# Weight-block sums issued behind the up projection's splits, and the last tile's mean behind the next tile's addition

## The chip, the cores and the metric

The kernel runs on one core of one Trainium2 chip. A core has five engines that each work through their own queue of instructions in order: PE (TensorE, matrix products), DVE (VectorE), ACT (ScalarE), POOL (GpSimd) and SP (SyncE, which here only issues transfers). They meet at semaphores. Transfers run on the core's 16 DMA engines; most are issued from SP's queue, some from POOL's and a few from ACT's. The metric is the device time of one execution in microseconds (us), as the median of several runs.

## The reference

One layer of a diffusion backbone over 512 latent tokens with 256 context tokens, model width 1024. What the change touches is the weights of the last part, the gated feed-forward network, and the final norm:

```python
def conv_ffn(h, w_up, conv_w, conv_b, w_down):
    u = dwconv_centred(h @ w_up, conv_w, conv_b)
    a, b = u[..., :D_FF], u[..., D_FF:]
    return (jax.nn.silu(a) * b) @ w_down
...
x = x + gt1 * o_lat
x = x + gt2 * conv_ffn(modulate(x, norm2_g[l], sh2, sc2), w_up[l], ...)
...
return rmsnorm(x, final_g)
```

`D_FF` is 2816, so `w_up` has 44 columns of 128-wide tiles (22 for `a`, 22 for `b`) and `w_down` has 22 rows of them. Ahead of it lie the modulation (six vectors from `silu(c) @ w_mod`), a combined input projection, a Mamba-2 scan in two directions, windowed attention of 16 heads, and the merge of both branches.

## The kernel before

**Products.** Every large product is made in float32r (a reduced form of float32 that PE takes at full rate) from operands that are split in two: `hi` is the rounded copy, `lo` the rest. `split` (L180) makes them from a raw weight tile: ACT casts `raw` to `hi` (L181), DVE subtracts to get `lo` (L182). `gemm` (L225) then issues three matmuls for each 128-row piece: hi with the operand's hi (L231), hi with its lo (L232), lo with its hi (L234). A weight tile of 128 x 1024 is 512 KB and 24 matmuls of 512 columns.

**Order of the stages.** The first norm and the input projection (0 to some 90 us) are followed by attention (to some 340 us), the scan (to some 700), the merge and the output projection (to some 870), the up projection (to some 1107), and the down projection to the end. In attention a planner writes out the order of PE, ACT and DVE by hand; its `product_atoms` (L1058) fill gaps with further input-projection tiles, whose split is `high` (ACT, L1081) and `low` (DVE, L1084). Elsewhere `run` (L204) walks a list of steps: for each it loads and splits the tiles of the steps ahead (`load`, L186), then calls the step. Weight tiles come through three raw buffers (`wraw`), two `whi` and two `wlo`.

**The up projection.** `up_step(t)` for t = 0 to 21 uses tile `("up", t)` for the gated half and `("up", 22 + t)` for the other, and applies the three-tap convolution and the gate (L1384 to L1386, L1892 to L1902). Between these steps `run` weaves in the last eight modulation tiles (`msteps[24:]`): they come through the same raw buffers, and DVE multiplies them by the conditioning vector straight from there (L787, L789). Others in between turn the residual stream around in memory for the last norm (`x1_turn`, L1950 and L1953, and `x1_load`, L1964).

**The down projection.** It is a product of two-by-two blocks, done with seven block products instead of eight (`down_step(j, u)`, j = 0 to 6). Four of the seven take not a block of `w_down` but a sum of blocks. These sums are made in device memory by transfers alone, `SUMS` at L149: for each of `DSUMS[4]`, `[1]`, `[2]`, `[5]`, in this order, four copies of 704 KB and then four accumulating transfers that add another block on top; two of the copies' sets read an earlier sum. They are issued from POOL's queue.

```python
    def sum_step(ins, n=1):

        for _ in range(min(n, len(SUMS))):
            o, x, how = SUMS.pop(0)
            dma = G.dma_start(o, x, **how)
            tc.add_manual_dep(dma.ins, ins.ins.name, BEHIND, reason="weight sums behind a split")
```

`sum_step` (L158) issues the next n of these 32 transfers and makes POOL wait for the instruction `ins`. Before the change, `ins` is the DVE subtraction of the g-th tile that fills attention (L1084): one transfer each for g = 0 to 3, two each for g = 4 to 11, one each for g = 12 to 23. The products that use the sums are j = 1 (`DSUMS[1]`), 2 (`[2]`), 3 (`[5]`) and 4 (`[4]`).

**The end.** The final norm is made for two tiles of 128 tokens, i = 0 and 1, out of the last block product. `near_last(i)` (L2066) multiplies each half of the product by its gate (L2070), adds it to the residual stream (L2072), has ACT square and sum it (L1996), and then takes the mean (`mean_root`: L2038 on DVE, a power on POOL, L2039). `near_out(i)` (L2076) scales (L2078 on ACT, L2082 on DVE) and stores. DVE and ACT keep the order written in `down_step`: near_last(0), near_last(1), near_out(0), near_out(1).

Of the kernel before, what the change touches and what calls it, by code (L numbers as in the profile page):

```python
# [13 lines left out]
ALU = mybir.AluOpType  # L14
# [10 lines left out]
NFF = 22  # L25
# [14 lines left out]
def raw(ap):  # L40
    return ap.bitcast(F32)
# [3 lines left out]
def tile_hybrid_layer(  # L45
# [32 lines left out]
    V, S, G, T = nc.vector, nc.scalar, nc.gpsimd, nc.tensor  # L78
# [28 lines left out]
    def accb():  # L107
        return bank("acc")

    def misb():  # L110
        return bank("mis")
# [3 lines left out]
    def tmp(tag):  # L115
        return tpool.tile([P, 512], F32, tag=tag, name=tag, bufs=TMP[tag])
# [27 lines left out]
    for j, t in enumerate((wdn[0], DSUMS[1], DSUMS[2], DSUMS[5], DSUMS[4], wdn[1], wdn[3])):  # L144
        for u in range(DU):
            n = min(2, DK - 2 * u) * HC
# [11 lines left out]
# [6 lines that stand above are left out]
# [3 lines left out]
    def load_raw(key):  # L167
        a, n = src[key]
        if key[0] == "dn" and key[1] >= 4 and key[1] % 2:
            if "dnraw" not in F:  # L170
                F["dnraw"] = hpool.tile([P, 4, 1024], F32, tag="hlh", name="dnraw")
            r = F["dnraw"][:, key[1] // 2 % 4, :]
        else:
            r = wpool.tile([P, 1024], F32, tag="raw", name="wraw", bufs=3)
        dma = nc.sync.dma_start(r[:, :n], a)
        if key[0] == "m":
            M_LOADS[key[1]] = dma
        return r, n

    def split(r, n, hi, lo):  # L180
        S.copy(hi[:, :n], r[:, :n])  # L181
        return V.tensor_tensor(lo[:, :n], r[:, :n], raw(hi[:, :n]), ALU.subtract)  # L182
# [3 lines left out]
    def load(key):  # L186
        r, n = load_raw(key)
        if key[0] == "m":
            return r
        if key in ELSEWHERE:  # L190
            hi, lo = ELSEWHERE[key]()
            split(r, n, hi, lo)
            return hi, lo
        if key[0] == "dn" and key[1] % 4 > 1:
            if "dnw" not in F:
                F["dnw"] = hpool.tile([P, 2, 2, 1024], F32R, tag="hll", name="dnw")
            hi, lo = (F["dnw"][:, key[1] % 2, i, :] for i in range(2))
        else:
            hi = wpool.tile([P, 1024], F32R, tag="whi", name="whi", bufs=2)
            lo = wpool.tile([P, 1024], F32R, tag="wlo", name="wlo", bufs=2)  # L200
        split(r, n, hi, lo)
        return hi, lo

    def run(prog, early=None):  # L204

        seq = [k for keys, _ in prog for k in keys]
        have, nload, nuse = {}, 0, 0
        for keys, fn in prog:
            nuse += len(keys)
            ahead = 1 + (early in keys) + any(k[0] == "dn" for k in keys)  # L210
            while nload < min(nuse + ahead, len(seq)):
                have[seq[nload]] = load(seq[nload])
                nload += 1
            fn(*[have.pop(k) for k in keys])
# [104 lines left out]
    class Plan:  # L319
# [6 lines left out]
        def add(self, name, engine, cost, needs, rank, emit, whole=True, load=0.11, late=False):  # L326


            self.atoms[name] = dict(
                name=name, engine=engine, cost=cost, needs=needs, rank=rank, emit=emit, whole=whole, load=load,  # L330
                late=late, start=None,
            )
# [86 lines left out]
    with tc.tile_pool(name="spool", bufs=1) as sp:  # L419
# [155 lines left out]
        def product(j, i, t):  # L575
            h = (hi_.get(j), lo_.get(j)) if j < NU else (hlh[:, j, :], hll[:, j, :])

            n = 3 * NU if j < NU else 3 * KT
            part(pg[i], ("P", i), n, [w[j][:, i * P : (i + 1) * P] if j in w else None for w in (wh, wl)], h, t)
# [75 lines left out]
        r = {}  # L655
        cq = tmp("te")[:, :LC]
        for j in range(KT):
# [46 lines left out]
            x = ("hi", "lo") if j >= NU else ("hh", "hl")  # L704
# [31 lines left out]
        for n in range(2):  # L736
            for j in range(KT):
                x = ("hi", "lo") if j >= NU else ("hh", "hl")
# [131 lines left out]
    Q, F = {}, {}  # L870
# [187 lines left out]
    def product_atoms(g, key, accs):  # L1058

        kind, t = key  # L1060
        d, R, G_ = {}, 1e6 + 100 * g, "%d" % g
# [19 lines left out]
            S.copy(d["w"][0], d["r"])  # L1081

        def low():
            sum_step(V.tensor_tensor(d["w"][1], d["r"], raw(d["w"][0]), ALU.subtract), 1 + (4 <= g < 12))  # L1084

        def rope_part(f):
            scale = -0.125 if kind == "k" else 1.0
# [37 lines left out]
        rw = R - 2e6 if g != 1 else -500  # L1125
        atom("w" + G_, "ACT", 1.05, was, rw, high, late=g > OLD)
        atom("v" + G_, "DVE", 1.225, ["w" + G_], rw, low, late=g > OLD)
        ks = range(-4 if kind == "k" else 0, 8)
        for k in ks:
# [31 lines left out]
        f = (q_high, q_low) if kind == "q" else (k_high, k_low)  # L1161
# [486 lines left out]
    for g in range(4):  # L1648
        s = ssd_steps(g)
        f = fill[n2 + g : n2 + 1 + g]  # L1650
        b = proj_steps(g + 1) if g < 3 else fill[n2 + 4 : n3]
# [104 lines left out]
    HL = L // 2  # L1756
    HALF = [slice(0, HL), slice(HL, L)]
# [110 lines left out]
    def f_split(s, ks, x):  # L1868
        S.copy(F["s"][s][:, 0, ks, :], x)
        V.tensor_tensor(F["s"][s][:, 1, ks, :], x, raw(F["s"][s][:, 0, ks, :]), ALU.subtract)  # L1870
# [99 lines left out]
    rows_ = {}  # L1970
# [17 lines left out]
    TWO = range(2)  # L1988

    def xq(h, i, c, z=slice(0, HC)):  # L1990

        return F["xt"][h][:, i, HC * c + z.start : HC * c + z.stop]

    def square_sum(h, i, col_, x):
        sq = tmp("ta")[:, : x.shape[-1]]
        S.activation(sq, x, AF.Square, scale=1.0 / 32.0, accum_out=ss[:, 2 * h + i, col_ : col_ + 1])  # L1996
# [39 lines left out]
    def mean_root(h, i, a, b, e):  # L2036
        ms, rs = (cpool.tile([P, 4], F32, tag=n, name=n, bufs=2)[:, 0:1] for n in ("ms", "rs"))
        V.scalar_tensor_tensor(ms, a, e, b, ALU.add, ALU.add)  # L2038
        G.tensor_tensor(rs, ms, phalf[:, 0:1], ALU.pow)  # L2039
        return rs  # L2040
# [22 lines left out]
        for i in TWO:  # L2063
            V.tensor_scalar_add(ss[:, i, 0:1], ss[:, i, 0:1], EPS)

    def near_last(i):  # L2066
        ps = F["A"][i]
        for b, z in enumerate(HALF):
            t = tmp("ta")[:, :HL]
            V.tensor_tensor(t, ps[:, z], rows_["g"][1][:, z], ALU.mult)  # L2070
            x = xq(0, i, 1, z)
            V.tensor_tensor(x, x, t, ALU.add)  # L2072
            square_sum(0, i, 1 + b, x)
        F["near", i] = mean_root(0, i, ss[:, i, 1:2], ss[:, i, 2:3], ss[:, i, 0:1])

    def near_out(i):  # L2076
        rs, r = F["near", i], P * i
        S.activation(F["p1"][i], F["p1"][i], AF.Copy, scale=rs)  # L2078
        S.dma_start(out[r : r + P, 0:HC], F["p1"][i])
        for z in HALF:  # L2080
            x = xq(0, i, 1, z)
            V.scalar_tensor_tensor(x, x, rs, rows_["f"][1][:, z], ALU.mult, ALU.mult)  # L2082
            nc.sync.dma_start(out[r : r + P, HC + z.start : HC + z.stop], x)
# [20 lines left out]
    def down_step(j, u):  # L2104
        tail = j == 6 and u == DU - 2

        def fn(*w):
            w = {u + n: x for n, x in enumerate(w)}
            if u == 0:
                if j == 0:  # L2110
                    F["A"] = [misb() for _ in TWO]
                F["ps", j] = F["A"] if j in CHAIN else [accb() for _ in TWO]
            ks = range(2 * u, DK if tail else min(2 * u + 2, DK))
            if tail:
                for i in TWO:
                    product(j, i, w, ks)
                with tc.manual_schedule(engines={mybir.EngineType.DVE, mybir.EngineType.Activation}):
                    for f in (near_last, near_out):
                        for i in TWO:
                            f(i)  # L2120
                return
            for k in ks:
                for i in TWO:
                    product(j, i, w, (k,))
            if 1 <= j < 6 and u < 4:
                z = slice(3 * u, min(3 * u + 3, DK))
                f_split((j + 1) % 2, z, OPERAND[j + 1]()[:, z, :])
            BESIDE_DOWN.get((j, u), lambda: None)()

        return [("dn", DU * j + u + n) for n in range(1 + tail)], fn  # L2130
# [99 lines left out]
```

## Time and profile before

| | |
|---|---|
| median of 3 runs | 1226.17 us (1224.75 to 1228.8) |
| the profiled execution's own time | 1223.88 us |
| its span from first to last instruction | 1222.1 us |
| granted TensorE clock | 0.998 of full speed |
| all transfers | 211.55 MB, mean 173 GB/s |
| of these POOL's queue (the 32 sums) | 23.07 MB, 8.5% of the 16 engines' span |
| SP's and ACT's queue q1 | 186.83 MB, 48.8% |

Times in a profile are counted from the start of the span. A row of a timeline is: start, duration, engine, line, operation, what it writes and reads, shape, and in brackets how long the engine had been idle and what released it. `SPq` and `POOL L162` rows of the kind DMA_DIRECT2D are issues of transfers: the duration is that of the issue, and a row "DMA to landing us min/median/max" tells how long the chosen transfers took from issue to landing. Rows of the form "A <- B: total, times, longest" tell how long engine A was idle until B released it.

### The profile page before, as it was taken

To read this page: it belongs to the slowest core of one execution; us is meant where nothing else is said; L and a number is where in the kernel's file an instruction comes from. 1 tells how busy PE (TensorE), PEld (TensorE's weight loads), DVE (VectorE), ACT (ScalarE), POOL (GpSimd) and SP (SyncE) were. 2 spreads that over 40 slices of the span, in tenths; PEclk is the share of its full clock that TensorE was granted. 3 is DMA by queue.
4 is the path that set the end of the run, shared out by engine and by line. 5 is a ranking of instruction groups with operands and counts; after the bars stand their busy time and mean duration, and the time that the engine had idled before them with its cause. 6 is when DMAs were issued, how large, how long until landed. Compare 5 with 4: busy or idle time off the path is not lost.

```text
span 1222.1 us, 17422 instructions
## 1 busy us (share of the span) xinstructions
PE 1210.9 (99%) x6310; PEld 994.8 (81%) x6310; DVE 919.6 (75%) x1481; ACT 682.7 (56%) x1275; POOL 196.2 (16%) x187
## 2 busy tenths in 40 slices
PE   9999999999999999999999999999999999999996
PEld 6798888888878877778777778888988888888885
DVE  5857888888654598697896868577787777777786
ACT  5658788787444467486575663223543434335653
POOL 0000121101000043352451631000200000000053
PEclk9999999999999999999999999999999999999999
DMA  9645789844754435346365568777266533347852
GB/s 372 255 137 183 160 252 256 173 153 125 174 160 151 129 104 176 109 133 195 102 176 194 159 214 273 230 249 224 56 149 162 167 107 103 120 125 181 290 162 87
DMA packets 122551, 211.55 MB, mean 173 GB/s; under 512 B 26720, under 2 KB 69024, under 8 KB 122464
## 3 DMA queue, kind: packets, MB, share of 16 engines
q1 hardware_dynamic: 111280, 186.83, 48.8%
q0 software_dynamic: 10752, 23.07, 8.5%
q8 instruction: 50, 0.82, 0.3%
q10 hardware_dynamic: 432, 0.53, 0.1%
q14 instruction: 37, 0.30, 0.1%
HBM read 185.68 MB, written 42.28 MB: 187 GB/s over the span
## 4 chain that ended last, share of the span: by engine, by line
PE 95%; ACT 1%; DVE 1%; POOL 1%; issue 1%; DMA 0%; POOLq 0%; DVEq 0%; ACTq 0%
PE acc L231 20%; PE acc L234 20%; PE acc L232 20%; PE score L951 3%; PE po L1000 3%; PE pt L987 2%; PE mis L573 2%; PE mis L1604 2%; PE mis L1497 2%; PE mis L2102 1%; PE mis L2100 1%; PE mis L2101 1%; PE mis L1612 1%; PE acc L1070 1%; PE acc L1072 1%; PE acc L1071 1%
## 5 line engine op out<-in xcount | busy, mean ns | idle before, releaser
L181 ACT CAST whi<-wraw 128x1024 fp32r<-128x1024 f32 (+1 forms) x115 | 120.3, 1047 | 157.4 <-PE acc L232 113.3
L231 PE MATMUL acc<-hlh,whi 128*128 128x512 f32 x472 | 194.1, 411 | 0.0
L182 DVE TENSOR_TENSOR wlo<-wraw,whi 128x1024 fp32r<-128x1024 f32 (+1 forms) x115 | 144.1, 1253 | 64.4 <-ACT whi L181 61.0
L232 PE MATMUL acc<-hll,whi 128*128 128x512 f32 x472 | 185.0, 392 | 0.0
L234 PE MATMUL acc<-hlh,wlo 128*128 128x512 f32 x472 | 185.0, 392 | 0.0
L231 PE MATMUL acc<-mh,whi 128*128 128x512 f32 x368 | 143.4, 390 | 0.0
L232 PE MATMUL acc<-ml,whi 128*128 128x512 f32 x368 | 143.2, 389 | 0.0
L234 PE MATMUL acc<-mh,wlo 128*128 128x512 f32 x368 | 143.2, 389 | 0.0
L234 PEld LDWEIGHTS acc<-hlh,wlo 128*128 128x128 f32 x472 | 88.6, 188 | 19.5
L231 PEld LDWEIGHTS acc<-hlh,whi 128*128 128x128 f32 x472 | 88.8, 188 | 17.9 <-issue 3.1
L232 PEld LDWEIGHTS acc<-hll,whi 128*128 128x128 f32 x472 | 88.9, 188 | 17.4 <-issue 2.4
L234 PEld LDWEIGHTS acc<-mh,wlo 128*128 128x128 f32 x368 | 69.1, 188 | 14.5
L231 PEld LDWEIGHTS acc<-mh,whi 128*128 128x128 f32 x368 | 69.1, 188 | 14.3
L232 PEld LDWEIGHTS acc<-ml,whi 128*128 128x128 f32 x368 | 69.1, 188 | 14.1
L1385 DVE SCALAR_TENSOR_TENSOR ta<-acc,half,ta 128x511 f32<-128x511 f32 (+1 forms) x66 | 43.9, 665 | 26.4 <-ACT ta L1384 26.0
L960 DVE CUSTOM_DVE_ANT_0 p<-score,winm,nsink 128x512 f32<-128x512 f32 (+1 forms) x64 | 51.9, 810 | 15.3 <-PE score L951 13.8
L1384 ACT ACTIVATE ta<-acc,half 128x512 f32<-128x512 f32 (+1 forms) x66 | 46.8, 709 | 22.8 <-PE acc L234 21.6
L967 ACT ACTIVATE p<-p,mneg 128x512 f32<-128x512 f32 (+1 forms) x64 | 49.7, 778 | 15.4 <-DVE mneg L960 14.8
L162 POOL DMA_DIRECT2D dsum<-wdn x24 | 25.4, 1143 | 193.0 <-DVE wlo L1084 171.7
L1499 POOL TENSOR_TENSOR st<-st,eT 128x512 f32<-128x512 f32 x24 | 29.7, 1239 | 165.4 <-ACT st L1516 152.0
L231 PE MATMUL acc<-hch,whi 128*128 128x256 f32 x176 | 54.7, 311 | 0.0
L995 DVE TENSOR_TENSOR ptl<-pt,pth 128x512 fp32r<-128x512 f32 x72 | 47.5, 685 | 8.5 <-ACT pth L991 7.9
(426 smaller groups left out, 2998.7 us busy)
## 6 DMA issues: line engine op xcount, KB each, us to landing
wraw<-wup SPq DMA_DIRECT2D x44, 512.0 KB, 3.6
dsum<-wdn POOLq DMA_DIRECT2D x24, 704.0 KB, 9.0
fb<-cs_d SPq DMA_DIRECT2D x32, 512.0 KB, 6.3
wraw<-wm SPq DMA_DIRECT2D x32, 512.0 KB, 3.7
wraw<-wx SPq DMA_DIRECT2D x24, 512.0 KB, 3.5
wm<-wm SPq DMA_DIRECT2D x16, 512.0 KB, 8.0
wraw<-wz SPq DMA_DIRECT2D x16, 512.0 KB, 3.6
wraw<-wos SPq DMA_DIRECT2D x16, 512.0 KB, 4.6
```

What stands on the lines that cost most here:

```text
L181: S.copy(hi[:, :n], r[:, :n])
L182: return V.tensor_tensor(lo[:, :n], r[:, :n], raw(hi[:, :n]), ALU.subtract)
L231: T.matmul(ps, wh, xh[:, k0 + k, :], start=a, stop=False)
L232: T.matmul(ps, wh, xl[:, k0 + k, :], start=False, stop=False)
L234: T.matmul(ps, wl, xh[:, k0 + k, :], start=False, stop=b)
L951: T.matmul(ps[:, o : o + len(z) * P], Q[h][:, b * P : (b + 1) * P], k[:, j, z[0] * P : (z[-1] + 1) * P], start=v == 0 and o % 512 in (0, P ...
L960: V.tensor_tensor_reduce(p[:, :w], d["ps"][i][:, o0 : o0 + w], m, op0=ALU.add, op1=ALU.min, scale=1.0, scalar=nsink[:, h : h + 1], accum_o ...
L967: S.activation(p, p, AF.Exp, bias=d["mneg"][:, i : i + 1], scale=-1.0, accum_out=d["den"][:, i : i + 1])
L995: V.tensor_tensor(d["ptl"][x], d["pt"][x], raw(d["pth"][x]), ALU.subtract)
L1000: T.matmul(d["po"], vst[:, cols[x], j, :], d[y][x], start=x == 0 and y == "pth", stop=x == c - 1 and y == "ptl")
L1384: S.activation(o[:, :n], ps[:, :n], AF.Identity, scale=hcol(base_w, stride + i), bias=hcol(base_b, i))
L1385: V.scalar_tensor_tensor(o[:, 1:n], ps[:, 0 : n - 1], hcol(base_w, i), o[:, 1:n], ALU.mult, ALU.add)
```

## The change

The sums leave attention's splits (`low`) and go behind the splits of up tiles t = 2 to 21, two at each of t = 2 to 13 and one at each of t = 14 to 21, in the same order. And `near_last` is cut into its two halves, with the mean as a step of its own: the mean of tile 0 now stands behind the first half of tile 1, the mean of tile 1 behind its second half.

```diff
--- before.py
+++ after.py
@@ -198,7 +198,9 @@
         else:
             hi = wpool.tile([P, 1024], F32R, tag="whi", name="whi", bufs=2)
             lo = wpool.tile([P, 1024], F32R, tag="wlo", name="wlo", bufs=2)
-        split(r, n, hi, lo)
+        low = split(r, n, hi, lo)
+        if key[0] == "up" and 2 <= key[1] < NFF:
+            sum_step(low, 2 if key[1] < 14 else 1)
         return hi, lo
 
     def run(prog, early=None):
@@ -1081,7 +1083,7 @@
             S.copy(d["w"][0], d["r"])
 
         def low():
-            sum_step(V.tensor_tensor(d["w"][1], d["r"], raw(d["w"][0]), ALU.subtract), 1 + (4 <= g < 12))
+            V.tensor_tensor(d["w"][1], d["r"], raw(d["w"][0]), ALU.subtract)
 
         def rope_part(f):
             scale = -0.125 if kind == "k" else 1.0
@@ -2063,14 +2065,14 @@
         for i in TWO:
             V.tensor_scalar_add(ss[:, i, 0:1], ss[:, i, 0:1], EPS)
 
-    def near_last(i):
-        ps = F["A"][i]
-        for b, z in enumerate(HALF):
-            t = tmp("ta")[:, :HL]
-            V.tensor_tensor(t, ps[:, z], rows_["g"][1][:, z], ALU.mult)
-            x = xq(0, i, 1, z)
-            V.tensor_tensor(x, x, t, ALU.add)
-            square_sum(0, i, 1 + b, x)
+    def near_last(i, b):
+        z, t = HALF[b], tmp("ta")[:, :HL]
+        V.tensor_tensor(t, F["A"][i][:, z], rows_["g"][1][:, z], ALU.mult)
+        x = xq(0, i, 1, z)
+        V.tensor_tensor(x, x, t, ALU.add)
+        square_sum(0, i, 1 + b, x)
+
+    def near_root(i):
         F["near", i] = mean_root(0, i, ss[:, i, 1:2], ss[:, i, 2:3], ss[:, i, 0:1])
 
     def near_out(i):
@@ -2115,9 +2117,9 @@
                 for i in TWO:
                     product(j, i, w, ks)
                 with tc.manual_schedule(engines={mybir.EngineType.DVE, mybir.EngineType.Activation}):
-                    for f in (near_last, near_out):
-                        for i in TWO:
-                            f(i)
+                    near_last(0, 0), near_last(0, 1)
+                    near_last(1, 0), near_root(0), near_last(1, 1), near_root(1)
+                    near_out(0), near_out(1)
                 return
             for k in ks:
                 for i in TWO:
```

## The prediction

> **What bounds the kernel now.** I read the page first, then the chain of waits, then three stretches of the span, then who waited for whom.
>
> ```profile
> span 1222.1 us, 17422 instructions
> PE 1210.9 (99%) x6310; PEld 994.8 (81%) x6310; DVE 919.6 (75%) x1481; ACT 682.7 (56%) x1275; POOL 196.2 (16%) x187
> PE 95%; ACT 1%; DVE 1%; POOL 1%; issue 1%; DMA 0%; POOLq 0%; DVEq 0%; ACTq 0%
> ...
> 0.72 3.98 DMA ccs<-cc
> ...
> 90.00:340.00 250.00, 249.94 (x1365) 213.57 (x1364) 200.97 (x410) 189.47 (x371) 29.64 (x32) 1.00 0.70 183
> 890.00:950.00 60.00, 60.00 (x267) 49.67 (x265) 46.90 (x69) 24.18 (x34) 0.00 (x0) 1.00 0.62 160
> 950.00:1100.00 150.00, 150.00 (x665) 124.21 (x664) 115.76 (x166) 59.98 (x81) 0.00 (x0) 1.00 0.38 122
> ```
>
> TensorE sets the end: 95% of the chain that ended last runs through it, and DMA has a share that rounds to 0. The stretch rows give PE, PEld, DVE, ACT and POOL busy time, granted clock, DMA share and GB/s. From 90 to 340 us (attention, where the sums run now) and from 890 to 1100 us (up projection, where they go) PE has no hole of more than 0.06 us. A busy PE need not be at its peak, so I checked the up projection by count: 665 matmuls in the last row's 150 us are 0.226 us each, 5.4 us for the 24 of a weight tile, with DVE idle for over a fifth of it. There is no hole to close there, only one to open.
>
> **The attention gives up the sums.** Thirty-two transfers of POOL's queue leave it.
>
> ```profile
> L162 POOL DMA_DIRECT2D dsum<-wdn x24: 515/1246/2132, 91.5 to 325.0; - x24
> ...
> DMA to landing us min/median/max: 4.7/8.1/16.6
> ...
> DMA to landing us min/median/max: 3.4/3.5/8.6
> ```
>
> The first row counts 24 of them; the other eight copy from an earlier sum. The first landing row is that of all the sums, the second that of the attention's weight loads (wraw, 90 to 340 us). Those loads do suffer: 8.6 us at worst against 3.5 at the median. But they are late for a split that PE isn't waiting for, as the 249.94 us of 250 say. What could be won at most: the chain's DMA share is below half a per cent, under 6.1 us, and its first step, the 3.98 us for ccs at the start, is in that share and stays; so at most 2.1 us. I take 0, since the row of the stretch itself leaves 0.06 us; bounds -2.1 and 0. On POOL the issues cost nothing either: 0.5 to 2.1 us each, they move to where POOL is idle (0.00 busy in both rows of the up projection) and nothing else stands in its queue. DVE and ACT issue the same instructions in the same order as before up to the last product, and SP's queue keeps its order throughout.
>
> **The up projection takes them.** Now the sums start behind the split of the first-half tile t: two each for t = 2 to 13, one each for t = 14 to 21. Each group of eight is four copies and then four accumulating transfers, so the pairs at t = 4, 5, 8, 9, 12 and 13 accumulate, and singles at t = 18 to 21 do. What they meet are SP's weight loads. How much a load is slowed by such a pair, attention shows:
>
> ```profile
> 136.44 2.50 POOL L162 DMA_DIRECT2D dsum<-wdn  x2 [10.19 <-DVE wlo L1084]
> DMA to landing us min/median/max: 9.4/10.8/12.2
> ...
> 137.54 0.40 SPq L175 DMA_DIRECT2D wraw<-wq  x1
> DMA to landing us min/median/max: 7.2/7.2/7.2
> ...
> DMA to landing us min/median/max: 7.2/7.7/8.1
> ...
> DMA to landing us min/median/max: 6.5/6.5/6.5
> ```
>
> A pair issued at 136.44 us lands after 9.4 and 12.2 us, and the 512 KB load issued among it takes 7.2. The last two rows are two loads at 174 to 189 us, beside two pairs (7.2 and 8.1), and one at 190.8 us that meets a pair's tail (6.5).
>
> For the up weights themselves that is hidden. The tightest that I found is the load at 951.41 us:
>
> ```profile
> 951.41 1.61 SPq L175 DMA_DIRECT2D wraw<-wup  x2
> DMA to landing us min/median/max: 3.5/3.5/3.5
> ...
> 959.26 1.05 ACT L181 CAST whi<-wraw 128x1024 fp32r<-128x1024 f32 x1 [3.61 <-PE acc L232]
> ...
> ACT whi L181 <- PE acc L232: 51.6, 34, 3.7
> ```
>
> It lands at 954.9 and its cast starts at 959.26, released by PE. With 8.1 us it would land at 959.5, 0.25 us late, and behind it lies more: the cast is released one tile ahead, so PE has 5.4 us until it needs the split, which takes 2.3. So 0. In the whole of the up projection the casts wait for PE (34 times), never for a wup load.
>
> It isn't hidden for the modulation loads (wm). They go through the same three raw buffers, and DVE reads them itself, in order, ahead of a split that PE needs:
>
> ```profile
> DVE tm L789 <- DMA wraw<-wm: 0.7, 3, 0.3
> ...
> 912.64 0.35 SPq L175 DMA_DIRECT2D wraw<-wm  x1
> 918.63 0.74 DVE L789 SCALAR_TENSOR_TENSOR tm<-wraw,csil,tm 128x512 f32<-128x512 f32 x1
> ...
> 960.35 1.22 DVE L182 TENSOR_TENSOR wlo<-wraw,whi 128x1024 fp32r<-128x1024 f32 x1 [0.80 <-ACT whi L181]
> 967.04 0.33 SPq L175 DMA_DIRECT2D wraw<-wm  x1
> DMA to landing us min/median/max: 3.4/3.4/3.4
> 970.50 1.54 DVE L789 SCALAR_TENSOR_TENSOR tm<-wraw,csil,tm 128x512 f32<-128x512 f32 x2
> 972.28 1.22 DVE L182 TENSOR_TENSOR wlo<-wraw,whi 128x1024 fp32r<-128x1024 f32 x1
> 976.06 0.39 PE L234 MATMUL acc<-mh,wlo 128*128 128x512 f32 x1
> ...
> 993.48 1.22 DVE L182 TENSOR_TENSOR wlo<-wraw,whi 128x1024 fp32r<-128x1024 f32 x1 [1.00 <-ACT whi L181]
> 1000.18 0.33 SPq L175 DMA_DIRECT2D wraw<-wm  x1
> DMA to landing us min/median/max: 3.6/3.6/3.6
> 1003.80 0.49 DVE L787 TENSOR_SCALAR tm<-wraw,csil 128x512 f32<-128x512 f32 x1 [0.35 <-DMA wraw<-wm]
> 1004.99 1.22 DVE L182 TENSOR_TENSOR wlo<-wraw,whi 128x1024 fp32r<-128x1024 f32 x1
> 1009.20 0.39 PE L234 MATMUL acc<-mh,wlo 128*128 128x512 f32 x1
> ```
>
> Four times already DVE waits a little for such a load (three at L789, one at L787). Take the load at 967.04: tile 9's split ends at 961.57, its accumulating pair starts there, and by the rows above it occupies the engines until about 974, so the load falls in its middle. DVE starts on it at 970.50, the moment it has landed (970.4). Queued behind is the split of tile 10, which ends at 973.50; PE's first product with that wlo starts at 976.06. The margin is 2.56 us. A landing of 7.2 instead of 3.4 us is 3.8 late, so PE stands still for 1.2 us (6.5: 0.5; 8.1: 2.1), and PE never gets back what it loses. The load at 1000.18 lies equally far behind tile 12's pair (994.70). Its split ends at 1006.21, PE needs it at 1009.20: margin 2.99. From 3.6 to 7.2 us is 3.6 late: 0.6 us (6.5: 0; 8.1: 1.5). Together I take 1.8 us, bounds 0.5 and 3.6. Why 7.2: it is the row with one accumulating pair and one load, as here.
>
> The other wm loads of this stage I take as 0. The one at 912.64 is first read at 918.63, 6.0 us after its issue, and a margin before PE comes on top; the one at 945.28 follows a pair of copies, which are shorter; the one at 1032.82 has one copy five us ahead of it; those at 1065.45 and 1087.22 meet the tail of one accumulating transfer. If the three of these with a transfer near them (945.28, 1065.45, 1087.22) took 8.1 us instead of the median 3.5, at the wider margin above, PE would stop 8.1 - 3.5 - 3.0 = 1.6 us at each: upper bound 4.8. The sums are ready in time: the last starts at 1093.4 and its block is the fourth product's, two products (over 50 us) into the down projection.
>
> In a sentence of its own: the Trainium skill, DMA: Bandwidth & Descriptors, section Queues, rings and completion order, has each DMA engine take turns between its queues packet by packet, which would let one foreign queue no more than double a load, 6.9 us from 3.45; by it the two stalls are 0.9 and 0.3 us and the sum below falls by 0.6. The rows of 7.2 to 8.1 lie above that, so they decide.
>
> **The last tile.** The second tile's first product moves ahead of the first tile's mean on DVE.
>
> ```profile
> 1210.49 0.39 PE L2102 MATMUL mis<-wlo,fs 128*128 128x512 f32 x1
> 1210.92 0.42 DVE L2070 TENSOR_TENSOR ta<-mis,rowssq 128x256 f32<-128x256 f32 x1 [3.98 <-PE mis L2102]
> ...
> 1212.53 0.39 PE L2102 MATMUL mis<-wlo,fs 128*128 128x512 f32 x1
> 1213.17 0.22 DVE L2038 SCALAR_TENSOR_TENSOR ms<-ss 128x1 f32<-128x1 f32 x1 [0.58 <-ACT ta L1996]
> 1213.31 0.42 DVE L2070 TENSOR_TENSOR ta<-mis,rowssq 128x256 f32<-128x256 f32 x1
> ```
>
> For the first tile DVE starts 0.43 us after the last matmul's start (1210.49 to 1210.92). So the second tile could start at 1212.96; it starts at 1213.31, since the mean ahead of it waits for ACT. That is 0.35 us. The mean isn't gone: it now stands between the second tile's two halves and takes the 0.14 us from 1213.17 to 1213.31 there. Net -0.2 us; bounds -0.35 and +0.14 (if the start doesn't move). What follows is unchanged.
>
> **Sum.** 0 - 0.2 + 1.2 + 0.6 = +1.6 us: the profiled execution's 1223.88 us (span 1222.1 and 1.8 around it) would become 1225.5. The median of the runs, 1226.17, lies 2.3 above that execution, and the forecast is set on it: 1227.8 us. All lower bounds together (-2.1, -0.35, +0.5) give -1.95, or 1224.2; all upper ones (0, +0.14, +3.6, +4.8) +8.5, or 1234.7.
>
> **Rivals.** *Hidden altogether*: the wm loads land by 6 us, within the margins. For it speaks that loads in attention mostly took 3.5; against it that each of the two falls in the middle of a pair. Time: -0.2, 1226.0. *The slow side*: wm loads behind accumulating transfers become what PE waits for all along the stage. Place: DVE's wait at L787 and L789; price: 3.6 us for the two, and 1.6 for each of two or three others, 6.8 to 8.4; it decides as soon as wm loads take over 7.5 us, which loads in attention did (8.1 and 8.6), and the stretch 890 to 950 already has a DMA share of 0.62 without the sums, against 0.70 in attention with them. Time about 1233. *Attention's relief*: if late loads there did cost PE, up to 2.1 us come back, with none lost: 1223.9. Against it stand PE's 249.94 us. *It doesn't do what it says*: the sums would have to start elsewhere; they hang on the splits named, and POOL has nothing queued in between, so I give it no chance.
>
> **How the numbers follow.** Forecast (+0.3 to +3.4): 0.45. Hidden: 0.19. Slow side: 0.28. Relief: 0.08. A measurement of this kernel can tell about 0.3%, 3.7 us, from no change: below 1222.5 is faster, above 1229.85 slower. The forecast and hidden cases lie within; the slow side lies beyond, and the relief stays within unless the runs scatter as those shown (1224.75 to 1228.8). Faster 0.06, same 0.65, slower 0.29. Range 1224.0 to 1232.5 us, which leaves out the worst of the slow side; the likeliest case alone has 1226.5 to 1229.6.
>
> **What would show it.** Right: PE's holes in the changed profile lie near 977 and 1009 us, about 1.2 and 0.6 us, ended by DVE's split at L182 (two lines further down in the new file); DVE waits for wm 3 to 4 us there; wup loads of 7 us without a wait of ACT. The attention keeps its 250 us. The second tile's product starts 0.35 us nearer to PE's last. Wrong: PE waits for ACT's casts, holes at more than three places, holes in the down projection behind a dsum load, or an attention shorter by over 1 us.

## The result, and the profile after

| | before | after |
|---|---|---|
| median of the runs | 1225.03 us (1224.2 to 1228.8, 19 runs) | 1230.0 us (1228.09 to 1232.11, 19 runs) |
| ratio of the paired runs | 1 | 1.0036, 95% interval 1.0029 to 1.0043 |
| profiled execution: time, span | 1223.88, 1222.1 us | 1230.0, 1228.2 us |
| granted TensorE clock | 0.998 | 0.997 |

The change costs 0.36%, 4.4 us (3.6 to 5.3 by the interval). That is just past the 0.3% that counted as no change, and it is more than the forecast's 1.6 us. The time lies inside the forecast range, but between two of its cases: above the likeliest (+0.3 to +3.4 us) and below the slow side (+6.8 to +8.4).

The page of the kernel after, with the rows that answer to those of before:

```profile
span 1228.2 us, 17424 instructions
PE 1213.1 (99%) x6310; PEld 995.1 (81%) x6310; DVE 916.6 (75%) x1481; ACT 682.2 (56%) x1275; POOL 197.2 (16%) x187
...
PE 87%; DVE 4%; DMA 4%; ACT 2%; issue 1%; POOL 1%; POOLq 0%; DVEq 0%; ACTq 0%
...
L236 PE MATMUL acc<-mh,wlo 128*128 128x512 f32 x368 | 143.6, 390 | 2.9 <-DVE wlo L182 2.9
```

PE's busy time has hardly moved (1210.9 to 1213.1), but its share of the chain of waits fell from 95% to 87%, and DMA's rose from 0 to 4%. The last row is new: in before PE never waited in the up projection; now 2.9 us of idle time stand before the matmul that reads wlo.

Three stretches of the kernel after (columns as in the prediction's stretch rows):

```profile
90.30:340.30 250.00, 249.93 (x1365) 213.56 (x1364) 200.55 (x409) 189.99 (x372) 0.00 (x0) 1.00 0.29 90
890.50:950.50 60.00, 60.00 (x266) 49.67 (x266) 46.16 (x67) 24.01 (x34) 8.29 (x10) 1.00 1.01 280
950.50:1110.00 159.50, 156.56 (x690) 128.61 (x689) 119.25 (x172) 61.74 (x85) 19.57 (x20) 1.00 0.78 212
```

In attention the DMA share fell from 0.70 to 0.29, and PE keeps its 249.9 us of 250: it gained nothing. In the up projection the share rose from 0.62 to 1.01 and from about 0.38 to 0.78, and PE lacks 2.94 us in the last row.

Where PE stops (its timeline, three rows of the kernel after):

```profile
955.61 0.50 PE L236 MATMUL acc<-mh,wlo 128*128 128x512 f32 x1 [0.53 <-DVE wlo L182]
...
979.04 0.50 PE L236 MATMUL acc<-mh,wlo 128*128 128x512 f32 x1 [1.37 <-DVE wlo L182]
...
1013.50 0.50 PE L236 MATMUL acc<-mh,wlo 128*128 128x512 f32 x1 [1.03 <-DVE wlo L182]
```

The brackets give idle time by modelled ends. I measured the loss in another way: each of the 6310 matmuls was set beside its counterpart in before, and where the difference of their starts (the shift) grows, PE lost time. The shift is 0.61 us ahead of the first place, 1.44 behind it, 3.11 behind the second and 4.47 behind the third: 0.83, 1.67 and 1.36 us lost, 3.86 in all. Of each, the matmul that was held back accounts for 0.69, 1.53 and 1.19 us. The other 0.13 to 0.17 us come in the matmuls right behind it (the next one starts 0.33 or 0.34 us after it, where 0.23 is usual). The expectations below, written during the study, give the first and the third loss as 0.76 and 1.32 us. The chain of waits of the kernel after names what each of the three waited for; a DMA row is the time of issue, the time to landing, and the transfer:

```profile
945.89 7.41 DMA wraw<-wm
...
969.30 6.65 DMA wraw<-wm
...
1003.29 7.72 DMA wraw<-wm
```

Two are the loads that the prediction named (967.04 and 1000.18 in before). The first, 945.28 in before, is one that it took as 0. PE's last matmul starts 6.27 us later than in before. Of that, 0.6 us come in the first 25 us and 1.75 us where the down projection begins (near 1122 us in before). Kernels without the sums' move show both as well (see the experiments).

What SP issues around that first load, in before:

```profile
940.42 0.81 SPq L1964 DMA_DIRECT2D xt<-x_d  x2
945.28 0.33 SPq L175 DMA_DIRECT2D wraw<-wm  x1
945.66 2.15 SPq L1964 DMA_DIRECT2D xt<-x_d  x2
```

and in the kernel after:

```profile
943.55 0.88 SPq L1966 DMA_DIRECT2D xt<-x_d  x2
945.89 0.33 SPq L175 DMA_DIRECT2D wraw<-wm  x1
946.27 1.26 SPq L1966 DMA_DIRECT2D xt<-x_d  x2
```

The first two reads of x_d stand 4.86 us ahead of the load in before and 2.34 us ahead in the kernel after, where tile 7's two copies (941.1 and 941.6 us) are in flight too.

Not every late load costs something. The modulation load of 913.25 us takes 8.76 us in the kernel after, the longest of all, and PE loses nothing there. An up load at 956.9 us takes 8.6 us, and ACT waits for no up weight; its row for the casts of this stage:

```profile
ACT whi L181 <- PE acc L234: 37.3, 23, 3.7
```

The end, on the timelines of PE and DVE:

```profile
1218.80 0.39 PE L2104 MATMUL mis<-wlo,fs 128*128 128x512 f32 x1
...
1219.30 0.42 DVE L2070 TENSOR_TENSOR ta<-mis,rowssq 128x256 f32<-128x256 f32 x1 [0.43 <-PE mis L2104]
1219.76 0.43 DVE L2072 TENSOR_TENSOR xt<-xt,ta 128x256 f32<-128x256 f32 x1
1220.10 0.21 DVE L2040 SCALAR_TENSOR_TENSOR ms<-ss 128x1 f32<-128x1 f32 x1
1220.23 0.42 DVE L2070 TENSOR_TENSOR ta<-mis,rowssq 128x256 f32<-128x256 f32 x1
```

The second tile's product starts 0.50 us after PE's last matmul, where it was 0.78. The first tile's mean (L2040) then takes 0.13 us between the halves. From PE's last start to the end of the span it is 9.42 us, 0.15 less than before.

### The profile page after: what moved, and what is told of

Same layout as the page of the kernel before. It is cut to its first block, busy times and chain, and to the rows that moved or that the text cites. A ratio compares the mean times of both kernels' runs of the same rounds, so it can differ in the third digit from the quotient of the medians.

```text
span 1228.2 us, 17424 instructions
## 1 busy us (share of the span) xinstructions
PE 1213.1 (99%) x6310; PEld 995.1 (81%) x6310; DVE 916.6 (75%) x1481; ACT 682.2 (56%) x1275; POOL 197.2 (16%) x187
## 4 chain that ended last, share of the span: by engine, by line
PE 87%; DVE 4%; DMA 4%; ACT 2%; issue 1%; POOL 1%; POOLq 0%; DVEq 0%; ACTq 0%
PE acc L233 18%; PE acc L236 17%; PE acc L234 17%; PE score L953 3%; PE po L1002 3%; DMA wraw<-wm 3%; PE pt L989 2%; PE mis L575 2%; PE mis L1606 2%; PE mis L1499 2%; DVE wlo L182 2%; PE mis L1614 1%; PE acc L1072 1%; PE acc L1074 1%; PE acc L1073 1%
## 5 line engine op out<-in xcount | busy, mean ns | idle before, releaser
L234 PE MATMUL acc<-hll,whi 128*128 128x512 f32 x472 | 185.0, 392 | 0.0
L236 PE MATMUL acc<-hlh,wlo 128*128 128x512 f32 x472 | 184.9, 392 | 0.0
L182 DVE TENSOR_TENSOR wlo<-wraw,whi 128x1024 fp32r<-128x1024 f32 (+1 forms) x115 | 143.4, 1247 | 54.5 <-ACT whi L181 50.0
L236 PE MATMUL acc<-mh,wlo 128*128 128x512 f32 x368 | 143.6, 390 | 2.9 <-DVE wlo L182 2.9
L234 PE MATMUL acc<-ml,whi 128*128 128x512 f32 x368 | 143.2, 389 | 0.0
L236 PEld LDWEIGHTS acc<-hlh,wlo 128*128 128x128 f32 x472 | 88.6, 188 | 19.5
L234 PEld LDWEIGHTS acc<-hll,whi 128*128 128x128 f32 x472 | 88.9, 188 | 17.4 <-issue 2.4
L236 PEld LDWEIGHTS acc<-mh,wlo 128*128 128x128 f32 x368 | 69.1, 188 | 18.5 <-DVE wlo L182 4.2
L234 PEld LDWEIGHTS acc<-ml,whi 128*128 128x128 f32 x368 | 69.1, 188 | 14.3
L791 DVE SCALAR_TENSOR_TENSOR tm<-wraw,csil,tm 128x512 f32<-128x512 f32 x56 | 43.9, 784 | 25.6 <-DMA wraw<-wm 24.9
```

Source lines behind the costliest of these rows:

```text
L234: T.matmul(ps, wh, xl[:, k0 + k, :], start=False, stop=False)
L236: T.matmul(ps, wl, xh[:, k0 + k, :], start=False, stop=b)
L791: V.scalar_tensor_tensor(acc, r[:, u * 512 : u * 512 + 512], sc, acc, ALU.mult, ALU.add)
```

## The experiments

Each kernel ran beside the kernel before on the same chip. Shifts are against the profiled execution of before. "Held back" is how much later the first matmul of a stop starts, against its counterpart, than the matmul ahead of it; "lost" is how much the shift has grown some 20 matmuls on.

### Each half of the change alone

The sums moved, the old tail:

```diff
-    def near_last(i, b):
...
+    def near_last(i):
...
+                    for f in (near_last, near_out):
+                        for i in TWO:
+                            f(i)
```

> Only the sums are moved, the last tile is as before. Theory (the modulation loads wm land late, DVE waits for them, PE stands at 954, 976, 1009 and about 1122 to 1129 us, 5.6 us in the profile of the change): the same holes, time 4.0 to 6.0 us above the kernel before, and 0.15 us above the changed kernel, which the clock can't tell. Rival (the new order at the end costs something too): 1 us or more below the changed kernel's 1230.

The new tail, the sums still behind attention's splits:

```diff
-        low = split(r, n, hi, lo)
-        if key[0] == "up" and 2 <= key[1] < NFF:
-            sum_step(low, 2 if key[1] < 14 else 1)
+        split(r, n, hi, lo)
...
+            sum_step(V.tensor_tensor(d["w"][1], d["r"], raw(d["w"][0]), ALU.subtract), 1 + (4 <= g < 12))
```

> Only the last tile's order is changed, the sums stay in attention. Theory: from PE's last start to the end 9.42 us instead of 9.57, no hole in the up projection, ratio 0.9999, within 0.1% of before. Rival (the order at the end costs): ratio above 1.001.

The sums alone: 1231.16 us, ratio 1.0048 (1.0030 to 1.0065). The tail alone: 1226.06, ratio 1.0007 (0.9998 to 1.0016). So the loss is the sums'; a gain of 0.15 us is too small for the runs to show. With the sums alone PE stops at the same three places (1.92, 1.83 and 1.12 us lost) and at one more (933.6 us, 0.54). With the tail alone it doesn't stop in the up projection, and yet loses 1.9 us where the down projection begins, much as the kernel after does.

### No sums at all, and before once more

```diff
-    for j, t in enumerate((wdn[0], DSUMS[1], DSUMS[2], DSUMS[5], DSUMS[4], wdn[1], wdn[3])):
+    for j, t in enumerate((wdn[0], wdn[2], wdn[2], wdn[0], wdn[0], wdn[1], wdn[3])):
...
-            sum_step(low, 2 if key[1] < 14 else 1)
+            pass
```

> The change with its own tail and no sums at all (the down projection reads blocks of its weight where it read the sums, as many bytes; the sums are left out of the computation). If the sums in the attention cost nothing, as was forecast: as the kernel with the sums in the attention and the new tail, 1225 to 1227 us, no holes in the up projection. If they cost something there that the change gives back: 1221 to 1224 us, and an attention that is shorter by 1 us or more.

> The kernel before, one more profiled execution. If what PE loses at the entry of the down projection (near 1122 us: 1.9 us more in two kernels of this study than in the profiled execution of before, one of them with its sums still in the attention) varies between executions of one program, this execution may show up to 2 us of it with the up projection unchanged. If it belongs to the new tail or to the sums' new place, this execution shows none.

The kernel without sums leaves out a part of the computation: its down projection reads blocks of `w_down` where it read the sums. It takes 1225.43 us, ratio 1.0003 (0.9994 to 1.0013). So to within the 0.1% of this interval the sums cost nothing where they were, and there was nothing to win by moving them. The second execution of before, and that of the kernel after, between 1110 and 1140 us; rows of who waited for whom: total, times, longest. First before:

```profile
PE acc L2100 <- ACT dnw L181: 1.2, 1, 1.2
PE acc L2102 <- DVE dnw L182: 0.5, 1, 0.5
```

and after:

```profile
PE acc L2102 <- ACT dnw L181: 0.7, 1, 0.7
PE acc L2104 <- DVE dnw L182: 0.5, 1, 0.5
```

Before loses 2.2 us there in its second execution, and PE doesn't wait there in its first: this stop comes and goes between executions of one program. The kernel without sums has it too (2.15 us). So it doesn't need the change, though I can't say how often each kernel has it. The first 25 us are 0.2 to 0.9 us longer in every profile than in the first one of before.

### The accumulating transfers as plain copies

```diff
-        SUMS += [(DSUMS[j][:, c], more[:, c], dict(accum_op=ALU.add, max_dma_last_dim=DK * P)) for c in cols]
+        SUMS += [(DSUMS[j][:, c], more[:, c], dict(max_dma_last_dim=DK * P)) for c in cols]
```

> The change with its own tail, where the 16 accumulating transfers are plain copies of the same shape at the same places (the second half of each sum is left out, its target is overwritten). Theory A, the accumulating ones are the dear ones: a transfer lands in about 5 to 7 us in place of 9 to 16.5, the wm loads at 967 to 970 and 1000 to 1003 us land in 4 to 5.5 us, the holes of 1.67 and 1.32 us go (0.3 us at most stays in each), and the median is 2 to 4 us under the change's, 1226 to 1228 us. Theory B, any block transfer beside the load is enough: the wm loads still take 6.5 us or more, both holes stay, 1229 us or more. The first hole (0.76 us near 954 us) stands beside plain copies already and should stay by both.

The second half of each sum is left out here. 1225.28 us, ratio 0.9999 (0.9990 to 1.0009): the loss is gone in the runs, and the median lies below the range of theory A. The four transfers from 955 to 966 us, first with the addition (the kernel after), then as copies:

```profile
L162 POOL DMA_DIRECT2D dsum<-wdn x4: 1245/1538/1807, 955.9 to 965.9; - x4
DMA to landing us min/median/max: 12.4/14.3/16.5
```

```profile
L162 POOL DMA_DIRECT2D dsum<-wdn x4: 745/750/777, 955.5 to 965.6; - x4
DMA to landing us min/median/max: 7.1/9.2/11.6
```

The copies aren't harmless, though. Two holes stay in the trace: 0.45 us lost at the first place and 1.07 at the second, where the load still lands 6.05 us after its issue. Theory A, which allowed 0.3 there, was wrong on that point; the third hole is gone. The 1.5 us of the trace lie just above the interval of the runs (up to 1.1 us); that difference stays open. The accumulating kind is what makes the loss large, not the only thing that makes a load late.

### One pair, on either side of a load

30 sums stay in attention. The last two, both accumulating, go behind tile 12 in one kernel and behind tile 13 in the other:

```diff
-        if key[0] == "up" and 2 <= key[1] < NFF:
-            sum_step(low, 2 if key[1] < 14 else 1)
+        if key[0] == "up" and key[1] in (12,):
+            sum_step(low, 2)
...
+            if g < 22:
+                sum_step(low, 1 + (4 <= g < 12))
```

> 30 of the 32 sums stay in the attention where they were; the last two, both accumulating, are issued together behind the split of the up projection's tile 12, some 5 us ahead of the modulation load of about 1000 us. The tail is the change's. Theory A, an accumulating pair a few us ahead of a wm load is enough by itself: that load lands in 6.5 us or more, PE has one hole in the up projection, 0.9 to 1.5 us near 1009 us before DVE's split of wlo, and no other there. Theory B, the load is late only because earlier sums have used up the distance of the buffers: no hole over 0.3 us. The median comes to within 2 us of before by both; the trace decides.

> As the kernel with the pair behind tile 12, with the same two accumulating sums behind tile 13, so that 15 us or more pass before the next modulation load. Theory A: no hole over 0.3 us in the up projection, wm loads land in 3.3 to 4 us, 1224.5 to 1227 us. If a pair in this stage costs something wherever it stands, a hole of 0.5 us or more follows in the 20 us behind it.

Medians: 1226.37 us (ratio 1.0007, 0.9998 to 1.0016) behind tile 12, 1225.13 us (0.9999, 0.9988 to 1.0009) behind tile 13. The traces tell more than the runs can. The modulation load of about 1000 us, with the pair behind tile 12:

```profile
L175 SPq DMA_DIRECT2D wraw<-wm x1: 328/328/328, 1000.6 to 1000.6; - x1
...
  DVE tm L789: 4.3, 1
...
DMA to landing us min/median/max: 7.6/7.6/7.6
```

and behind tile 13:

```profile
L175 SPq DMA_DIRECT2D wraw<-wm x1: 328/328/328, 1001.0 to 1001.0; - x1
...
  DVE tm L789: 0.2, 1
...
DMA to landing us min/median/max: 3.5/3.5/3.5
```

With the pair 4 to 5 us ahead of it (995.5 and 996.3), the load takes twice as long, DVE waits 4.3 us for it, and PE loses 1.2 us at 1010.7 us. One tile later (1007.2 and 1008.0) the pair stands behind this load, 25 us ahead of the next one, and costs PE nothing in the whole up projection. A single pair at the wrong place is enough; no pile of earlier sums is needed.

### No sums behind tile 7

```diff
-            sum_step(low, 2 if key[1] < 14 else 1)
+            sum_step(low, 0 if key[1] == 7 else 2 if key[1] < 16 else 1)
```

> The change, but no sums are issued behind tile 7, ahead of the modulation load of about 945 us; the later ones move back by one tile, so that the accumulating pairs stand behind tiles 4, 5, 9, 10, 13 and 14 and plain pairs behind 11 and 12. In the change the load of 945 us was issued on time and landed late, beside two plain copies and four reads of x_d. Theory A, what lies in flight beside the load when it is issued decides: the 945 us load lands in 5.5 us or less and the hole of 0.76 us near 954 us goes (0.3 us at most), the hole near 976 us stays (1 to 2 us, an accumulating pair ahead of it), that near 1009 us falls to 0.5 us or less (plain pairs ahead of it); 1226.5 to 1229 us. Theory B, the distance that the accumulating pairs behind tiles 4 and 5 used up comes due at tile 7's load, whatever is beside it: the 945 us load is issued a us or more late or the hole stays at 0.7 us or more.

1226.51 us, ratio 1.0022 (1.0010 to 1.0033), at the lower edge of theory A's range. The load of 945.88 us lands after 5.4 us and its hole is gone; plain copies now stand ahead of the load of 1001.83 us, which lands after 3.9 us, and that hole is gone too. The one with an accumulating pair ahead of it stays, 1.06 us; its row of PE's timeline:

```profile
977.58 0.50 PE L236 MATMUL acc<-mh,wlo 128*128 128x512 f32 x1 [0.77 <-DVE wlo L182]
```

The runs lose 2.7 us (1.2 to 4.0 by the interval), more than this one hole. The traced execution, 1226.04 us, is the fastest of the seven; what the others lose besides isn't known.

### Pairs beside the loads' tiles

```diff
-        if key[0] == "up" and 2 <= key[1] < NFF:
-            sum_step(low, 2 if key[1] < 14 else 1)
+        if key[0] == "up" and key[1] in (2, 3, 5, 6, 8, 10, 11, 13, 14, 16, 17, 19, 21):
+            sum_step(low, 2)
...
+            if g < 6:
+                sum_step(low)
```

> The change with its own tail; six of the 32 sums (the first of the attention's splits) stay in the attention, and the other 26 go in pairs behind the splits of the up projection's tiles 2, 3, 5, 6, 8, 10, 11, 13, 14, 16, 17, 19 and 21, so that no pair is issued in the tile's time in which a modulation tile's load (wm) is issued (the loads follow the splits of tiles 4, 7, 9, 12, 15, 18 and 20 by some 5 us). Theory A, a wm load is late only because a pair of sums was issued a few us ahead of it: the wm loads land in 3.4 to 5.5 us, the three holes of 0.76, 1.67 and 1.32 us in the up projection go, and the median comes to within 1.5 us of before (ratio 1.000 to 1.0012). Theory B, the holes come of the sums' traffic in the whole of this stage, wherever it is issued: wm loads still take over 6 us at two places or more, holes of 2 us or more in sum, 1228 us or more. What is lost at the entry of the down projection varies between executions and tells nothing here.

1229.01 us, ratio 1.0032 (1.0020 to 1.0044): theory A missed, though no wm load has a pair in its own tile. From 970 us on it holds, and nothing is lost in the up projection. But there is one long hole at the first place: the matmul is held back 2.88 us, and 4.6 us are lost in all (the last section comes back to the difference). SP's timeline there:

```profile
937.90 2.95 SPq L1957 DMA_DIRECT2D x_d<-te  x3
941.94 0.94 SPq L175 DMA_DIRECT2D wraw<-wup  x1
946.90 1.82 SPq L1968 DMA_DIRECT2D xt<-x_d  x2
948.77 0.42 SPq L175 DMA_DIRECT2D wraw<-wm  x1
```

and what SP and PE waited for in the up projection of this kernel, one row each:

```profile
SPq L1968 <- DMA x_d<-te: 3.8, 1, 3.8
```

```profile
PE acc L236 <- DVE wlo L182: 2.7, 1, 2.7
```

The accumulating pair here stands behind tile 6 (933.1 us), and lands up to 11.9 us later. It falls on the stores of x_d, which land 7.9 to 8.1 us after issue, up to 946.8 us; in before they took 3.7 to 4.0. The reads of x_d have to wait for them, and the modulation load stands behind these reads in SP's queue: it is issued at 948.77, 3.0 us late, and takes 6.57 us besides. A load can thus be late in two ways, by a long way to landing and by a late issue, and a pair some 15 us ahead of it can do the second.

### The last sums out of the attention's way, where they cost nothing

```diff
-            sum_step(low, 2 if key[1] < 14 else 1)
+        if key[0] == "up" and key[1] in (13, 14, 16, 17, 19, 21):
+            sum_step(low, 2)
...
+            if g < 20:
+                sum_step(low)
```

> 20 sums one by one in the attention, the other 12 in pairs behind tiles 13, 14, 16, 17, 19 and 21 of the up projection: behind the stretch in which this stage also stores and reads x_d, and never in the tile's time of a modulation load. The tail is the change's. Theory A: no hole over 0.3 us in the up projection, and the time of before within 1.5 us (1224 to 1226.5 us, ratio 0.9992 to 1.0010); no gain either, since the sums cost PE nothing in the attention. If taking 12 transfers out of the attention frees something there, it is under 1224 us and the attention is shorter by 0.5 us or more. If pairs cost PE here too, 1227 us or more.

1225.02 us, ratio 0.9998 (0.9989 to 1.0006). No hole in the up projection, with eight accumulating transfers in it, and no gain. No kernel of the study beats before.

### Two that told little

The sums spread otherwise, to have none near the down projection:

```diff
-            sum_step(low, 2 if key[1] < 14 else 1)
+            sum_step(low, 2 if key[1] < 17 else 1 if key[1] in (17, 21) else 0)
```

> The changed kernel, with no sums behind tiles 18 to 20: two each behind 2 to 16, one behind 17, and the last still behind 21. The last two wm loads then meet no sum, while the last sum runs beside the down projection's first loads as in the change. Theory (the entry's hole, 1.9 us, is DVE's lateness from the last wm loads): it goes, 954, 976 and 1009 stay, time 1.5 to 2 us below the changed kernel. Rival (the last sum itself slows the down projection's loads): the entry's hole stays, time as the changed kernel within 0.7 us.

1230.77 us, ratio 1.0052 (1.0030 to 1.0075). The stop at 1122 us is absent, a similar one of 1.2 us comes at 1133 (both in the time of before); since before has or lacks it too, that decides nothing. In the up projection the three holes stay, and 1.4 us are lost near 934 us besides.

The modulation tiles loaded into a buffer of their own kind, not the three raw ones:

```diff
+        elif key[0] == "m" and key[1] >= 24:
+            if "dnraw" not in F:
+                F["dnraw"] = hpool.tile([P, 4, 1024], F32, tag="hlh", name="dnraw")
+            r = F["dnraw"][:, key[1] % 4, :]
```

> The changed kernel, with the eight modulation tiles of the up projection loaded into buffers of their own (the four that the down projection uses later) instead of the three raw buffers. SP reaches their issue 4 to 5 us earlier. Theory (what costs is DVE's wait for wm): the holes at 954, 976 and 1009 go, and the one at the down projection's entry too, if it came from DVE's lateness; time within 1 us of before, ratio 0.999 to 1.001. Rival (traffic of the sums in itself: last sums beside the down projection's first loads): the three holes go, 1 to 2 us stay at the entry, ratio 1.001 to 1.002. Rival (the up weights are late as well, or POOL's issues disturb): 3 us or more stay.

1251.87 us, ratio 1.0214. The memory that these tiles took over is in use until the up projection ends, so the loads were only issued at 1115 to 1128 us, and PE lost some 21 us behind them (and 8.6 more near 930 us, where DVE waited 9.8 us for a store of x_d). It says nothing of a free buffer; whether loads issued further ahead would close the holes wasn't tried.

## Why the prediction was right and wrong

**Attention gives 0: right.** PE has 249.93 of 250 us with the sums gone, and the kernel without any sums is no faster.

**Late modulation loads stop PE: right, in kind and place.** Two of the holes are where it put them, ended by DVE's split of wlo, and ACT never waited for an up weight. The estimate of 7.2 us to landing stands beside 6.65 and 7.72 us measured. At 1000 us the longer landing accounts for the matmul being held back 1.19 us instead of 0.6. That the load of 912.64 us (913.25 in the kernel after) has room enough was right as well: it took 8.76 us and cost nothing. A slip in the signs: L182 keeps its number in the new file; it is the matmul's L234 that becomes L236.

**"The other wm loads of this stage I take as 0": the step that failed.** For the load at 945.28 us the reason was that it "follows a pair of copies, which are shorter". It does, but it also runs beside four reads of x_d, and with both it took 7.41 us. Without the copies, in the kernel with no sums behind tile 7, it took 5.38 and cost nothing, though the reads stood as near to it. The prediction's upper bound did hold 1.6 us for this load; the sum took 0. The load held the matmul back 0.69 us itself, and it cost the next load something as well. The prediction worked each stall out as if all before it were on time. DVE started on the first load's product 3.6 us late (953.33 us, where 949.09 moved by the shift of 0.61 would be 949.70), caught up in part, and still freed the raw buffer of the next load 0.82 us late: in the kernel after that load is issued at 969.30, where 967.04 moved by the shift of 1.44 would be 968.48. Hence the matmul there was held back 1.53 us instead of 1.2, although the load took 6.65 us and not 7.2. A third, smaller thing had no term: each stop loses 0.13 to 0.17 us more in the matmuls behind it.

With issue and landing both counted, the prediction's own margins hold to 0.06 us in every kernel that I worked out. The time that a matmul is held back is the delay of the load's issue, plus the landing beyond that of before (3.79, 3.43 and 3.60 us), minus the margin. The delay of an issue is counted against before, moved by PE's shift at that point. The margins of 2.56 and 2.99 us are the prediction's; that of the first load, 2.93, is fitted to the kernel after and tested on the others.

| load, kernel | issue late | to landing | worked out | held back |
|---|---|---|---|---|
| 945, after | 0.00 | 7.41 | fitted | 0.69 |
| 945, all copies | 0.00 | 7.03 | 0.31 | 0.32 |
| 945, none behind tile 7 | 0.00 | 5.38 | 0 | 0 |
| 945, beside the loads' tiles | 3.03 | 6.57 | 2.88 | 2.88 |
| 967, after | 0.82 | 6.65 | 1.48 | 1.53 |
| 967, all copies | 0.82 | 6.05 | 0.88 | 0.93 |
| 967, none behind tile 7 | 0.00 | 6.86 | 0.87 | 0.93 |
| 1000, after | 0.00 | 7.72 | 1.13 | 1.19 |
| 1000, pair behind tile 12 | 0.00 | 7.59 | 1.00 | 1.05 |
| 1000, all copies | 0.00 | 4.53 | 0 | 0 |

The three loads of the kernel with the sums alone come out as 1.77, 1.63 and 0.91 us, against 1.77, 1.69 and 0.97 measured; those of the sums spread otherwise as 2.02, 0.40 and 0.82, against 2.02, 0.46 and 0.88. The row "967, all copies" also explains why copies alone left a hole there: without the 0.82 us handed on by the load before, 0.06 would be left of it.

**The Trainium skill** (DMA: Bandwidth & Descriptors, Queues, rings and completion order) has each DMA engine take turns between its queues. The prediction took from it a bound of 6.9 us for a load. Four of the ten loads in the table lie above that (7.03 to 7.72 us), six below, and the one of 913.25 us (8.76) lies above it too; so it is no bound here.

**The tail: right.** -0.15 us against -0.2; the second tile's product came 0.28 us nearer to PE's last start, where 0.35 was expected.

**The sum.** The terms measured are 0.83 + 1.67 + 1.36 - 0.15 = 3.7 us in the profiled execution, against +1.6. The runs say +4.4 (3.6 to 5.3), which covers the 3.7; whether more than these terms is at work isn't shown. That the median came within 2.2 us of the forecast 1227.8 owes something to luck: the forecast was set on a median of three runs, 1226.17, and that of 19 runs of the same kernel is 1225.03. The slow-side rival had the right thought (more loads than two) and too high a price: it counted on four or five holes from loads of over 7.5 us, and there are three, one of them from such a load; the other load of over 7.5 us (8.76 at 913.25) made no hole.

## What to carry to other kernels

A transfer that is off the path isn't free where it goes: ask which loads of the new stage are consumed straight from the buffer with the least time between landing and use, and keep heavy transfers out of the few us ahead of them. Count a stall by issue and landing together, in order of time, since a late load delays the release of a buffer, and a store that lands late holds up whatever is queued behind its reader. And where the profile says that a stage has no hole, expect nothing of taking traffic out of it; here it won nothing.

## What the runs showed of the hardware

**The price of accumulation.** At the same place a 704 KB transfer between two places in device memory landed after 12.4 to 16.5 us when it added to its target, and after 7.1 to 11.6 us as a copy; its issue took 1.2 to 1.8 us instead of 0.75.

**A long stop of PE costs more than the stop.** In the kernel with one pair behind tile 12, PE stood for 2.11 us at the entry of the down projection, and 0.53 us again. The stretches that follow, by the same columns (granted clock third from the end):

```profile
1120.00:1126.00 6.00, 3.94 (x18) 2.93 (x16) 0.00 (x0) 1.04 (x2) 0.00 (x0) 1.00 0.78 100
1126.00:1128.00 2.00, 1.42 (x4) 0.89 (x5) 1.97 (x2) 2.00 (x3) 0.00 (x0) 0.83 0.56 171
1128.00:1130.00 2.00, 2.00 (x6) 1.56 (x5) 2.00 (x3) 2.00 (x4) 0.00 (x0) 0.50 0.97 151
1130.00:1132.00 2.00, 2.00 (x9) 1.60 (x8) 2.00 (x3) 1.80 (x3) 0.00 (x0) 0.81 0.98 353
1132.00:1136.00 4.00, 4.00 (x19) 3.31 (x18) 3.20 (x5) 2.31 (x3) 0.00 (x0) 1.00 1.03 412
```

The granted clock falls to 0.50, and matmuls start 0.43 us apart instead of 0.23. The three rows below full clock lack 0.17, 0.50 and 0.19 of 2 us each, 1.7 us together, which at 0.50 is 3.4 us of half rate. The same happened behind the 2.7 us stop of the kernel with pairs beside the loads' tiles (granted clock 0.56 and 0.59 in the 4 us after it). There 4.6 us were lost where the matmul was held back 2.88; the 1.7 us between fall on the matmuls at half rate behind it. It happened behind two stops of 1.85 us as well, in the kernel of the sums spread otherwise (0.50 from 960 to 962 us) and in that of the sums alone (0.50 from 1130.3 to 1133.7 us). From 20 us on, no stop of 1.61 us or less was followed by it in any profile here (that of 1.61 us is the one at 957 us with the sums alone).

The Trainium skill, TensorE: Matmul & The Clock Gate, section What's actually happening, names the two states, full and half rate, and a window of some 3.4 us without work as what leads to the lower one. Here stops of 1.85 to 2.7 us were enough, and half rate lasted about as long as the window that it names.
